# A decoder trunk on one core: treated K pairs in both output projections and in the attention's values

## The chip, the cores and the metric

The kernel runs on one core of a Trainium2 chip. The metric is device time in microseconds of one execution, as the median of several. Engines are named as in the profile: PE (TensorE, matmuls), PEld (its weight loads), DVE (VectorE), ACT (ScalarE), POOL (GpSimd) and SP (SyncE, which issues most DMAs).

## The reference

Two decoder layers over 256 tokens of width 2048, all in float32. Layer 0 mixes with a state space scan (SSD), layer 1 with differential attention; each is followed by a SwiGLU FFN, and every sub-layer has an RMSNorm before and after it.

```python
for i in range(DEPTH):                      # DEPTH = 2
    h = rmsnorm(x, norm_mix_pre[i])
    if i % 2 == 0:
        m = ssd_mixer(h, ssd_w_in, conv..., dt_bias, a_log, d, ssd_norm, ssd_w_out)
    else:
        m = diff_attention(h, da_w_qkv, lambdas..., da_subln, da_w_out, lambda_init)
    x = x + rmsnorm(m, norm_mix_post[i])
    h = rmsnorm(x, norm_ffn_pre[i])
    x = x + rmsnorm((silu(h @ w_gate) * (h @ w_up)) @ w_down, norm_ffn_post[i])

# the end of ssd_mixer: a gated RMSNorm in 8 groups, whose gain stands before the product
return (gv * rsqrt(mean(gv * gv) + eps) * norm_w) @ w_out          # 4096 -> 2048
# diff_attention: 16 heads, value width 128
q, k, v = split(u @ w_qkv)                                          # 2048 -> 3 x 2048
pr = softmax(q0 k0) - lam * softmax(q1 k1);  o = pr @ v
return (rmsnorm(o, subln_w) * (1 - lambda_init)) @ w_out            # 2048 -> 2048
```

## The kernel before

**Products.** Every matmul operand is split into a high part `hi` (float32r, a cast on ACT) and a low part `lo` (the rest, a subtraction on DVE). A product is three matmuls: high by high, high by low, low by high. `prep` (L126) splits a block of weights after its DMA, with a scale where one is given (L137, L138), else plainly (L133, L134). Weights come in blocks of 512 rows (four K tiles of 128) by 512 columns, 1 MB; a "chunk" is 512 output columns, a "K pair" two K tiles. The 256 tokens are two row tiles, t = 0 and 1.

**Three forms of a product.** `mv` (L177) does one chunk: the activations are stationary and the weights move; row tile 1 runs `lag` steps behind row tile 0 and the rest is carried over into the next product through the queue `pending`. `ws` (L201) has the weights stationary and gives the transposed result; queries and keys use it. `pair` (L220) does two chunks at once. In it, the K pairs named in `seven` are "treated": the four quarter products (2 row tiles by 2 chunks) of two K tiles are put together from seven products in place of eight, after a scheme of sums and differences. Such a K pair needs `form`s, that is sums and differences of the activations (`make_form`, L817: eight 128x128 operations on DVE and a split), and sums and differences of the weights: an accumulating DMA from the POOL queue (L247) and three additions on DVE (L261 to L263), then a second `prep`. Its extra products are gathered in four PSUM banks of the pool `auxp` (`cp` in the profile) and put together on DVE after the last treated K pair (L275 to L280). Before, the FFNs alone use `pair`, with K pairs 2, 4 and 6 treated for gate and up (`SEVEN`) and the lists in `PARTS` for the down projection.

**Order of work.** The emitted order is also the priority of the scheduler that lays out each engine's stream; it may let work that is ready go ahead of work that waits. `later(k, fn)` puts a piece of side work k steps on, `tick` counts steps, `lookup` runs such pieces early where their result is needed, and `flush` empties `pending`.

**The stages that the change touches.** The SSD output projection (`out_proj` with `w_so`) runs in two halves of K: the first half of all four chunks in the middle of the scan (L786), chunk 0 of the second half at its end (L788), and chunks 1 to 3 after the scan's pools are closed and others are opened (L848). Its activations are the pieces of `gate_group` (L615; `act_piece` transposes and splits them). The gain `ssd_norm` is applied to the weights. The last chunk ends in `norm_chain` (L642), which makes the residual and the next `xT`, the transposed activations, one row tile at a time; the sums of squares of the other chunks, with a product by the norm's gain on POOL (L688), are made by `sums` when a chunk is done.

In attention (L967), for each of four groups of four heads (`hg`): values by `mv`, then queries and keys by `ws`, then softmax and the rest as side work (`later`) under the next group's products. Value tiles lie in the pool `mpool` with two buffers. The output projection (L1071) is four chunks by `mv`.

Raw weight blocks have three buffers (`rawp`); while `deep` is set, in the FFN's middle, two of five go to `mpool` as well. The split tiles `hi` and `lo` have four buffers each.

## Time and profile before

| | |
|---|---|
| median of 3 runs | 2540.5 us (2540.33 to 2541.4) |
| profiled execution | 2541.16 us, span 2539.4 us |
| granted TensorE clock | 0.998 |
| PE busy | 2517.3 us, 11866 matmuls |
| DVE, ACT, POOL busy | 1901.7, 1364.6, 224.4 us |
| DMA | 536.16 MB, mean 211 GB/s |

The span reaches from the first instruction to the last; the profiled execution's time has 1.76 us around it. Busy time of PE is the union of overlapping matmuls, so it tells where TensorE had work, not at what pace. `acc`, `cp`, `hi`, `lo`, `raw` are tiles by the program's names, `ah_s`/`al_s`, `ah_f`/`al_f` and `ah_o`/`al_o` the high and low parts of the SSD's, the FFN's and the attention's activations. In time, the scan with the first half of the output projection takes the first 612 us, the rest of the output projection and the norm lie up to about 717 us, the first FFN up to about 1426, attention up to about 1759, its output projection and norm up to about 1825, and the second FFN the rest.

### The profile page before, as it was taken

The page shows a single profiled execution, that of the slowest core. Times are in us where ns is not written, and L with a number is a line of the kernel's source. Part 1 is how long each engine was busy: PE and PEld are TensorE (multiplying, and loading weights), DVE is VectorE, ACT ScalarE, POOL GpSimd, SP SyncE. Part 2 cuts the span into 40 slices and gives each one's busy share as a digit, 9 for nine tenths or more (in the row PEclk, how much of TensorE's full clock was granted, in tenths as well). Part 3 has the DMA queues.
Part 4 walks back from the last instruction along what each step waited for, and adds up shares of the span by engine and source line. Part 5 has one row for each costly group of instructions (what it writes and reads, how often), then busy time and mean ns, then how long its engine had stood idle before and what let it go on. Part 6 is the DMA issues. An engine that isn't in the chain of part 4 may idle for free.

```text
span 2539.4 us, 31214 instructions
## 1 busy us (share of the span) xinstructions
PE 2517.3 (99%) x11866; PEld 2071.8 (82%) x11866; DVE 1901.7 (75%) x2274; ACT 1364.6 (54%) x1655; POOL 224.4 (9%) x214
## 2 busy tenths in 40 slices
PE   9999999999999999999999999999999999999998
PEld 7877888788888888888888888887888888888886
DVE  6777547777687888977887765566688889878985
ACT  5767546665565454544454654455655454535453
POOL 0121000110110000001001100001100000010002
PEclk9999999999999999999999999999999999999999
DMA  7545555554776776778677544544666966796673
GB/s 279 197 167 183 186 194 199 166 183 171 257 261 211 254 238 210 235 230 244 209 239 243 189 150 166 183 151 156 241 222 201 292 213 214 234 264 207 211 251 146
DMA packets 141366, 536.16 MB, mean 211 GB/s; under 512 B 14176, under 2 KB 30880, under 8 KB 114208
## 3 DMA queue, kind: packets, MB, share of 16 engines
q1 hardware_dynamic: 125584, 502.91, 57.3%
q0 software_dynamic: 15264, 30.94, 6.4%
q8 instruction: 93, 1.52, 0.2%
q14 instruction: 57, 0.47, 0.1%
q10 hardware_dynamic: 368, 0.32, 0.0%
HBM read 516.22 MB, written 17.89 MB: 210 GB/s over the span
## 4 chain that ended last, share of the span: by engine, by line
PE 91%; DVE 3%; issue 2%; ACT 2%; DMA 1%; POOL 0%; SPq 0%; DVEq 0%; ACTq 0%; POOLq 0%
PE acc L238 36%; PE acc L187 35%; PE cp L238 7%; PE acc L212 5%; PE acc L214 2%; DVE lo L134 2%; ACT hi L133 1%; PE sc L1010 1%; PE pt_f L291 1%; PE py L565 1%; DMA mt<-acum_d 1%; PE ptx L658 0%; PE po L1046 0%; PE pc L472 0%; PE pt_s L291 0%
## 5 line engine op out<-in xcount | busy, mean ns | idle before, releaser
L134 DVE TENSOR_TENSOR lo<-raw,hi 128x2048 fp32r<-128x2048 f32 (+2 forms) x451 | 848.2, 1888 | 363.0 <-ACT hi L133 362.2
L133 ACT CAST hi<-raw 128x2048 fp32r<-128x2048 f32 (+2 forms) x451 | 699.9, 1558 | 592.0 <-DVE raw L263 189.2
L238 PE MATMUL acc<-hi,xT 128*128 128x512 f32 x1840 | 589.0, 390 | 0.0
L187 PE MATMUL acc<-hi,xT 128*128 128x512 f32 x1792 | 586.1, 399 | 0.6 <-ACT hi L133 0.5
L238 PEld LDWEIGHTS acc<-hi,xT 128*128 128x128 f32 x1840 | 345.3, 188 | 71.5
L187 PEld LDWEIGHTS acc<-hi,xT 128*128 128x128 f32 x1792 | 335.8, 188 | 74.1 <-issue 4.9
L238 PE MATMUL acc<-lo,xT 128*128 128x512 f32 x920 | 358.1, 389 | 0.0
L187 PE MATMUL acc<-lo,xT 128*128 128x512 f32 x896 | 352.3, 394 | 2.6 <-DVE lo L134 2.6
L133 ACT CAST hi<-rawm 128x2048 fp32r<-128x2048 f32 (+1 forms) x115 | 207.8, 1807 | 173.7 <-DVE rawm L263 108.3
L134 DVE TENSOR_TENSOR lo<-rawm,hi 128x2048 fp32r<-128x2048 f32 (+1 forms) x115 | 248.1, 2157 | 70.2 <-ACT hi L133 66.1
L238 PEld LDWEIGHTS acc<-lo,xT 128*128 128x128 f32 x920 | 172.7, 188 | 35.7
L187 PEld LDWEIGHTS acc<-lo,xT 128*128 128x128 f32 x896 | 169.0, 189 | 40.2 <-DVE lo L134 5.5
L238 PE MATMUL acc<-hi,ah_f 128*128 128x512 f32 x468 | 183.1, 391 | 0.0
L238 PE MATMUL acc<-hi,al_f 128*128 128x512 f32 x468 | 182.2, 389 | 0.0
L238 PE MATMUL acc<-lo,ah_f 128*128 128x512 f32 x468 | 182.1, 389 | 0.0
L212 PE MATMUL acc<-xT,hi 128*128 128x512 f32 x512 | 180.4, 398 | 0.0
L238 PE MATMUL cp<-hi,ff 128*128 128x512 f32 x468 | 156.8, 389 | 0.0
L214 PE MATMUL acc<-xT,lo 128*128 128x256 f32 x512 | 143.0, 280 | 0.0
L138 DVE SCALAR_TENSOR_TENSOR lo<-raw,cols,hi 128x512 fp32r<-128x512 f32 x128 | 92.5, 769 | 56.6 <-ACT hi L137 56.3
L137 ACT ACTIVATE hi<-raw,cols 128x512 fp32r<-128x512 f32 x128 | 84.6, 715 | 59.4 <-PE acc L187 39.3
L212 PEld LDWEIGHTS acc<-xT,hi 128*128 128x128 f32 x512 | 96.1, 188 | 22.8
L238 PEld LDWEIGHTS acc<-hi,al_f 128*128 128x128 f32 x468 | 87.8, 188 | 18.3
(279 smaller groups left out, 3469.9 us busy)
## 6 DMA issues: line engine op xcount, KB each, us to landing
raw<-in_w_zxbc_dram SPq DMA_DIRECT2D x77, 1024.0 KB, 4.8
raw<-in_w_d_dram SPq DMA_DIRECT2D x98, 512.0 KB, 5.8
raw<-in_w_g_dram SPq DMA_DIRECT2D x96, 512.0 KB, 6.0
raw<-in_w_u_dram SPq DMA_DIRECT2D x96, 512.0 KB, 5.8
raw<-in_w_qkv_dram SPq DMA_DIRECT2D x48, 1024.0 KB, 4.7
raw<-in_w_so_dram SPq DMA_DIRECT2D x32, 1024.0 KB, 4.8
rawm<-in_w_g_dram SPq DMA_DIRECT2D x64, 512.0 KB, 5.9
rawm<-in_w_u_dram SPq DMA_DIRECT2D x64, 512.0 KB, 6.0
```

The source lines that it names most:

```text
L133: nc.scalar.copy(hi, raw)
L134: nc.vector.tensor_tensor(lo, raw, hi.bitcast(F32), op=ALU.subtract)
L137: nc.scalar.activation(hi[:, j], raw[:, j], AF.Copy, scale=scale[j])
L138: nc.vector.scalar_tensor_tensor(lo[:, j], raw[:, j], scale[j], hi[:, j].bitcast(F32), op0=ALU.mult, op1=ALU.subtract)
L187: nc.tensor.matmul(acc[t], a, b[:, j], start=(i == 0 and j == 0 and q == 0), stop=(i == last and j == 1 and q == 2))
L212: nc.tensor.matmul(acc[ct], hi[:, j, cs], x.rearrange("p a s -> p (a s)"), start=(i == 0 and j == 0), stop=False)
L214: nc.tensor.matmul(acc[ct][:, :S], lo[:, j, cs], x[:, 0], start=False, stop=(i == last and j == 1))
L238: nc.tensor.matmul(acc[k], a, b, start=first and q == 0, stop=last and q == 2)
L291: nc.tensor.transpose(pt[:, j], src[:, j * P:(j + 1) * P], ident)
L565: nc.tensor.matmul(py[e * 64:(e + 1) * 64, a], xd[c][:, 2 * a + e], mts[c][:, 2 * a + e], start=True, stop=True)
L1010: nc.tensor.matmul(sc[c][:, h], qT[cp, h % 2, ts], kT[cp, h % 2, :nk * P], start=True, stop=True)
```

## The change

1. `ssd_norm` is no longer applied to the weights: `prep`, `halves` and `mv` lose their scale, and `act_piece` applies the gain to the transposed activations instead, in four operations of 128 columns on ACT and on DVE each (in place of one of 512).
2. In both output projections chunks 1 and 2 become a `pair` with three treated K pairs: 9, 11, 13 of 8 to 15 in the SSD's second half, 1, 3, 5 of 0 to 7 in the attention's. Chunk 0 goes before it and chunk 3 after it by `mv`. Their forms are made as side work of chunk 0 and lie in `xT`, which is idle at that time (`idle_xT`).
3. The values are made by `v_pair`, two groups at a time, with K pairs 4 and 6 treated: groups 0 and 1 ahead of the first queries, groups 2 and 3 between the third group's queries and its keys. The two forms are made in the first and used in both; they lie in a buffer of `mpool`. In the first, row tile 1 of K pairs 0 and 1 comes after row tile 0 of both (`lead`).
4. In these pairs the first sum of the weights is an addition on DVE (`chip`) in place of the accumulating DMA.
5. In a pair of the output projections, the sums of chunk 0 are made three steps into it and the third gain load follows one step later; the partial sum `p3` moves from the third chunk's end to wherever the third sum is made.

```diff
-    def prep(raw, scale=None):
+    def prep(raw):
...
+        nc.scalar.copy(hi, raw)
+        nc.vector.tensor_tensor(lo, raw, hi.bitcast(F32), op=ALU.subtract)
         return hi, lo
...
-    def pair(blocks, stat, seven, form, done):
+    def pair(blocks, stat, seven, form, done, lead=0, chip=False):
...
-            if kp in seven:
-
+            if kp in seven and chip:
+                nc.vector.tensor_tensor(raw[:, 0], raw[:, 0], raw[:, 1], op=ALU.add)
+            elif kp in seven:
                 nc.gpsimd.dma_start(raw[:, 0:1], src[0][:, 1:2], accum_op=ALU.add)
             if kp not in seven:
                 hi, lo = prep(raw)
-                for t in range(NT):
+
+                def block(t, kp=kp, hi=hi, lo=lo):
                     for c, e in ((0, 2), (1, 0)):
                         for j in range(2):
                             mm((t, c), stat(kp, j, t), hi[:, e + j], lo[:, e + j], kp == end and j == 1)
                         if kp == end:
                             done(t, c, acc[(t, c)], ss)
                     tick()
+
+                block(0)
+                if kp < lead:
+                    pending.append(lambda block=block: block(1))
+                    if kp == lead - 1:
+                        flush()
+                else:
+                    block(1)
                 continue
...
+        for sl in (slice(0, 4),) if scale.shape[1] == 1 else [slice(j, j + 1) for j in range(4)]:
+            sc = scale if scale.shape[1] == 1 else scale[:, sl]
+            nc.scalar.activation(hi[:, sl], pt[:, sl], AF.Copy, scale=sc)
+            nc.vector.scalar_tensor_tensor(lo[:, sl], pt[:, sl], sc, hi[:, sl].bitcast(F32),
+                                           op0=ALU.mult, op1=ALU.subtract)
...
+    def idle_xT(i):
+
+        return xT[i // 2][:, :, :, i % 2 * P:(i % 2 + 1) * P]
...
-            ssd_act[(t, g)] = act_piece(yf, f"s{g}_{t}")
+            ssd_act[(t, g)] = act_piece(yf, f"s{g}_{t}", scale=ssd_norm[:, 4 * g:4 * g + 4])
...
+            if 1 in two:
+
+                later(3, lambda: [row(t, 0) for t in range(NT)])
+                later(4, lambda: pw(2))
...
+                if first and last:
+                    nc.vector.tensor_tensor(m[k], ps, y, op=op)
+                    return
...
-    out_proj(w_so, False, False, ssd_act, list(range(8, 16)), 0, False, 1, None, None, ssd_norm, ns=range(0, 1))
+    sforms = {}
+    for k, kg in enumerate((9, 11, 13)):
+        later(2 + 2 * k, lambda k=k, kg=kg: make_form(
+            sforms, kg, act_stat(ssd_act), lambda name, shape: s2.tile(list(shape), F32, tag="t2", name=name), at=idle_xT(k)))
+    out_proj(w_so, False, False, ssd_act, list(range(8, 16)), 0, False, 1, None, None, ns=range(0, 1))
...
-    out_proj(w_so, False, True, ssd_act, list(range(8, 16)), 0, False, LAG2, t512, load_post(0), ssd_norm, ns=range(1, 4))
+
+    out_proj(w_so, False, True, ssd_act, list(range(8, 16)), 0, False, LAG2, t512, load_post(0), ns=(3,),
+             two={1: (9, 11, 13)}, forms=sforms)
...
+    def v_pair(hg, seven, lead=0):
+
+        def done(t, c, ps, ss):
+            if not c and not t:
                 vt = mpool.tile([P, 4, 512], F32, tag="m", name="v")
...
+            y, op = ss[(t, c)]
+            nc.vector.tensor_tensor(y, ps, y, op=op)
+            nc.scalar.activation(values[(hg + 1 - c, t)], y, AF.Copy, scale=lookup(rstd, (1, t)))
+
+        pair(twos(w_qkv, 8 + hg), kp_stat, seven, lambda kp, f: form_of(lookup(vforms, kp), f), done, lead, True)
...
+    for k, kp in enumerate((4, 6)):
+        later(6 + 3 * k, lambda k=k, kp=kp: values_forms(k, kp))
+    v_pair(0, (4, 6), LAG // 2)
...
     for hg in range(4):
+        attention_keys(hg, 0)
+        if hg == 2:
+
+            v_pair(2, (4, 6))
+        attention_keys(hg, 1)
         attention_group(hg)
-    out_proj(w_ao, True, True, att, list(range(8)), 2, False, LAG2, t512, load_post(2))
+    aforms = {}
+    for k, kg in enumerate((1, 3, 5)):
+        later(3 + 2 * k, lambda k=k, kg=kg: make_form(aforms, kg, act_stat(att), t512, at=idle_xT(k)))
+    out_proj(w_ao, True, False, att, list(range(8)), 2, False, LAG2, t512, None, ns=(0,))
+    out_proj(w_ao, True, True, att, list(range(8)), 2, False, LAG2, t512, load_post(2), ns=(3,),
+             two={1: (1, 3, 5)}, forms=aforms)
```

141 lines of the change are left out of this document (69 added, 72 removed).

## The prediction

> **What bounds the kernel now.** I read the parts of the page first, then the cores, the chain of work, the groups by form, and the windows of the stages that the change touches.
>
> ```profile
> PE 2517.3 (99%) x11866; PEld 2071.8 (82%) x11866; DVE 1901.7 (75%) x2274; ACT 1364.6 (54%) x1655; POOL 224.4 (9%) x214
> core 0: 2539.4 us, clock 0.998
> L238 PE MATMUL acc<-hi,xT 128*128 128x512 f32 x1840 | 589.0, 390 | 0.0
> 1894.04 6.12 PE acc L238 x27
> 624.12 73.49 PE acc L187 x324
> 1426.37 12.00 PE acc L187 x52
> 1438.36 0.44 PE pb L312 x4
> PE acc L187 <- DVE lo L134: 2.6, 5, 1.3
> ```
>
> PE is busy for all but 22 us of the span, at full clock, so TensorE's stream is the bound and a saving has to come out of it. The group row says 390 ns for a matmul, but neighbours overlap: the chain (start, length, count) passes 27 matmuls of L238 in 6.12 us and 324 of L187 in 73.49 us, both 0.227 us each. One matmul taken out is worth 0.227 us, not 0.390. A stage stays on that pace only while VectorE (DVE) and ScalarE (ACT) hand over the high and low parts in time; the last row shows that L187 waited for a low part only 2.6 us in the whole run.
>
> The windows give start:end, length, then busy time (and count) of PE, PEld, DVE, ACT, POOL, then clock, DMA share, GB/s.
>
> ```profile
> 832.60:874.00 41.40, 41.40 (x193) 34.43 (x192) 36.56 (x47) 17.61 (x14) 2.84 (x4) 1.00 0.72 246
> 612.00:633.50 21.50, 21.50 (x100) 17.79 (x99) 17.27 (x28) 17.00 (x29) 1.58 (x2) 1.00 0.57 185
> 633.50:675.00 41.50, 41.50 (x184) 34.35 (x183) 26.06 (x36) 22.87 (x40) 5.90 (x4) 1.00 0.81 304
> 1406.00:1431.30 25.30, 24.17 (x118) 18.59 (x117) 23.37 (x57) 21.33 (x57) 4.56 (x6) 1.00 0.46 166
> 1431.30:1459.00 27.70, 27.70 (x154) 24.05 (x153) 15.85 (x10) 13.74 (x9) 0.44 (x1) 1.00 0.64 228
> 1570.00:1612.00 42.00, 42.00 (x224) 34.32 (x224) 28.70 (x49) 24.45 (x48) 2.02 (x2) 1.00 0.38 131
> 1750.00:1800.00 50.00, 50.00 (x234) 41.28 (x233) 23.51 (x21) 23.58 (x27) 11.49 (x7) 1.00 0.52 185
> ```
>
> The first row is a pair of chunks in the FFN with three treated K pairs, as the change now makes elsewhere: DVE is busy 36.56 of 41.40 us and PE misses nothing. The second and third are the SSD output projection, the fourth is the norm between the first FFN and attention, where DVE is busy 23.37 of 25.30 us, the fifth the time in which the first values pair would finish, the sixth the third values chunk and what follows, the seventh the attention's output projection.
>
> **The matmuls.** A plain K pair over two chunks is 2 row tiles x 2 chunks x 2 K tiles x 3 products = 24 matmuls; a treated one is 7 x 3 = 21. Treated pairs added: three in the SSD output projection, three in the attention's, two in each of two values pairs: 10. 10 x 3 = 30 matmuls, 30 x 0.227 = 6.81 us off TensorE. Nothing else is added to PE: forms, chip additions and scales are on DVE and ACT.
>
> **What a treated pair costs beside PE.**
>
> ```profile
> L134 DVE TENSOR_TENSOR lo<-raw,hi 128x2048 fp32r<-128x2048 f32 x241 | 551.0, 2294 | 247.6 <-ACT hi L133 246.9
> L133 ACT CAST hi<-raw 128x2048 fp32r<-128x2048 f32 x241 | 458.8, 1912 | 410.9 <-DVE raw L263 189.2 <-PE acc L212 85.0 <-issue 40.5
> L134 DVE TENSOR_TENSOR lo<-raw,hi 128x1536 fp32r<-128x1536 f32 x50 | 87.6, 1752 | 18.9 <-ACT hi L133 18.9
> L133 ACT CAST hi<-raw 128x1536 fp32r<-128x1536 f32 x50 | 74.2, 1483 | 67.2 <-PE acc L238 39.2 <-issue 14.4 <-ACT hi L133 7.1
> L263 DVE TENSOR_TENSOR raw<-raw 128x512 f32<-128x512 f32 x50 | 34.2, 684 | 0.0
> L824 DVE TENSOR_TENSOR xf<-xT 128x128 f32<-128x128 f32 x24 | 5.3, 283 | 0.0
> L285 DVE TENSOR_TENSOR ff<-f,ff 128x512 fp32r<-128x512 f32 x18 | 12.3, 687 | 2.4 <-ACT ff L284 2.4
> 1016.58 2.29 DVE L134 TENSOR_TENSOR lo<-rawm,hi 128x2048 fp32r<-128x2048 f32 x1 [2.11 <-ACT hi L133]
> 1018.78 2.28 DVE L134 TENSOR_TENSOR lo<-raw,hi 128x2048 fp32r<-128x2048 f32 x1
> ```
>
> Plain pair on DVE: 2.29 us. Treated: 0.68 (the chip addition that stands in for the accumulating DMA) + 1.75 + 3 x 0.68 + 2.29 = 6.78 us. A form: 8 x 0.283 + 0.69 = 2.95 us. The last two rows, of a timeline, show the hole in a treated pair: before the second low part DVE waits 2.11 us for ACT's second cast. They also show a low part issued 2.20 us after the last one, so the 2.29 overlap a little.
>
> **First values pair.** Before, the four blocks of values 0 are 96 matmuls, and PE has them done when L312 starts at 1438.36.
>
> ```profile
> 1420.18 2.28 DVE L134 TENSOR_TENSOR lo<-raw,hi 128x2048 fp32r<-128x2048 f32 x1
> 1430.80 0.61 DVE L664 SCALAR_TENSOR_TENSOR xT<-ptx,cols,xT 128x128 fp32r<-128x128 f32 x2 [0.43 <-ACT xT L663]
> ```
>
> The fourth block's low part is made at 1420.18, and xT is complete at about 1431.3. In the new pair K pairs 0 to 3 are also 96 matmuls, so PE comes to treated pair 4 near 1438.4 and wants pair 6's second low part 21 + 24 + 9 = 54 matmuls later, at 1450.6. From 1431.3 DVE has 19.3 us for two forms (5.9), two treated pairs (13.6) and a plain one (2.3): 21.8, of which the 1.9 us that DVE idles in the fourth window could take some. So 19.9 in 19.3: 0.6 late, and two holes of 2.11 make it 4.8 late if nothing fills them. The overlap of neighbouring instructions (about 0.08 on some 30) pulls it the other way, to nothing. I take 1.5 late, nearest to the FFN row, where the holes are mostly filled, and keep 0 and 4.8. The queries behind it need only one low part at first. The shorter lead (2 K pairs of row tile 0 = 24 matmuls, 5.4 us, instead of five halves = 30, 6.8 us) is covered by K pair 2's row tile 0 if that is placed ahead; if not it costs up to 1.4, inside the same range. The second values pair has no forms to make and the sixth row leaves DVE 13 us idle: nothing. Moving the third queries ahead of it puts the second group's softmax under a queries product instead of under the pair; both keep PE full, nothing. Its two half loads per K pair cost SP one more issue:
>
> ```profile
> raw<-in_w_so_dram SPq DMA_DIRECT2D x32, 1024.0 KB, 4.8
> raw<-in_w_d_dram SPq DMA_DIRECT2D x98, 512.0 KB, 5.8
> wpost<-in_post_rows_dram SPq DMA_DIRECT2D x16, 256.0 KB, 4.9
> ```
>
> A K pair lands in 5.8 us with three buffers ahead of PE's 4.8 to 5.4 us each: nothing. The third wpost load now sits on SP behind the POOL product of row 0, with the next K pairs' loads queued after it; its cover is the K pairs already loaded (two, over 10 us): nothing, and up to its 4.9 us if they were used up.
>
> **SSD output projection.**
>
> ```profile
> L138 DVE SCALAR_TENSOR_TENSOR lo<-raw,cols,hi 128x512 fp32r<-128x512 f32 x128 | 92.5, 769 | 56.6 <-ACT hi L137 56.3
> L137 ACT ACTIVATE hi<-raw,cols 128x512 fp32r<-128x512 f32 x128 | 84.6, 715 | 59.4 <-PE acc L187 39.3 <-issue 13.1 <-DMA raw<-in_w_so_dram 7.0
> L134 DVE TENSOR_TENSOR lo<-raw,hi 128x1024 fp32r<-128x1024 f32 x160 | 210.4, 1319 | 96.5 <-ACT hi L133 96.4
> L664 DVE SCALAR_TENSOR_TENSOR xT<-ptx,cols,xT 128x128 fp32r<-128x128 f32 x96 | 27.8, 345 | 5.3 <-ACT xT L663 5.1
> L663 ACT ACTIVATE xT<-ptx,cols 128x128 fp32r<-128x128 f32 x96 | 29.3, 374 | 9.4 <-PE ptx L658 8.3 <-DVE xT L664 0.3
> L285 DVE TENSOR_TENSOR al_s<-pt_s,ah_s 128x512 fp32r<-128x512 f32 x16 | 10.9, 683 | 2.2 <-ACT ah_s L284 2.2
> L284 ACT CAST ah_s<-pt_s 128x512 fp32r<-128x512 f32 x16 | 9.3, 578 | 0.0
> ```
>
> The scale leaves the weights: a block of four on DVE falls from 4 x 0.77 = 3.08 to 2 x 1.32 = 2.64 us (2.29 where it is one piece), on ACT from 4 x 0.715 = 2.86 to about 2. It goes to 16 activation pieces, priced by the nearest shape: DVE 4 x 0.345 = 1.38 for 0.68, ACT 4 x 0.374 = 1.50 for 0.58. None of it is on PE's path before (no L138 in PE's waits), so the relief is worth nothing there; the added 0.7 and 0.9 us per piece can delay a low part in the scan: 0 to 1, I take 0.2.
>
> Chunk 0 also makes three forms: 17.27 + 8.9 - 4 x 0.44 + two late pieces 1.4 = 25.8 us of DVE for 21.5, a backlog of 4.3 if none is made in earlier idle time, 0 if all is. The pair then asks 5 x 2.29 + 3 x 6.78 + 4 x 0.68 = 34.5 us of 41, less than the FFN row's 36.56, which PE did not feel. I take 1.0, range 0 to 4.3. The attention's projection has the same pair, but the seventh row leaves DVE half idle for the forms: 0.1, up to 1.5.
>
> **A lock that speaks against it.** Row sums end in a POOL product (L688, 1.30 us); row 0's two now fall into the pair.
>
> ```profile
> 1376.79 3.80 POOL L688 TENSOR_TENSOR m<-m,wpost 128x512 f32<-128x512 f32 x3 [4.78 <-ACT junk L302]
> 1379.77 5.17 DVE L134 TENSOR_TENSOR lo<-raw,hi 128x2048 fp32r<-128x2048 f32 x2 [3.82 <-ACT hi L133]
> 1780.95 2.29 DVE L134 TENSOR_TENSOR lo<-raw,hi 128x2048 fp32r<-128x2048 f32 x1 [3.63 <-ACT hi L133]
> 1781.61 2.79 POOL L688 TENSOR_TENSOR m<-m,wpost 128x512 f32<-128x512 f32 x1 [7.17 <-ACT junk L302]
> ```
>
> Where the two meet, one waits: three POOL products alone take 3.80, but one begun under a low part takes 2.79, and two low parts behind a product take 5.17 instead of 4.49. If both products come first in each output pair, DVE loses 2 x 1.3 us per pair; at 34.5 + 2.6 = 37.1 of 41 that is at the FFN row's load, so I add nothing in the sum and keep it as a rival. The Trainium skill states this rule (SBUF — State Buffer, Who interferes with whom): a DVE instruction with two SBUF inputs and a GpSimd one that reads SBUF take turns at a shared port pair, each holding it for a whole instruction. The trace agrees, by the 2.79 and 5.17.
>
> **Sum.** -6.81 + 1.5 + 1.0 + 0.2 + 0.1 = -4.0 us. The profiled execution took 2541.16 us (span 2539.4 and 1.76 around it), the median of the runs is 0.66 lower: 2540.5 - 4.0 = 2536.5.
>
> **Rivals.** (a) *All of it is kept*: late parts cost under 1.7, 2533.7 to 2535.4. For it: the FFN row, with no PE wait at 88% DVE, and DVE idle for 11.9 of 27.7 us in the fifth window. Against: that idle time is what the forms and treated pairs fill. Chance 0.36. (b) *Partly given back*, the forecast, 2535.4 to 2540.5. Chance 0.43. (c) *The port pair takes the rest*: 2 x 2.6 us on top of the late parts in the two output pairs, so -4.0 + 5.2 = +1.2, 2541.7; it decides if DVE has no slack when row 0's products run. Chance 0.11. (d) *The treated pair is a serial chain*: cast 1.48, low part 1.75, additions 2.05, cast 1.91, low part 2.29 and the next plain pair's 2.29 make 11.8 us for PE's 10.2 (45 matmuls); 10 times 1.6 = 16 late, 2540.5 - 6.8 + 16 = 2549.7, slower. It decides from 1.2 us per treated pair on (11.9 in all). Against it: 1018.78 follows 1016.58 without a hole, and the FFN runs this pattern unhindered. Chance 0.10.
>
> About 0.2% (5.1 us) is what a measurement of this kernel can tell from no change: faster is below 2535.4, slower above 2545.6. Faster is (a), 0.36; slower most of (d), 0.09; same the rest, 0.43 + 0.11 + 0.01 = 0.55. The range goes from the full saving with a microsecond of old waits gone, 2532.8, to just past (c), 2542.5; that leaves out (d) and a little at either end. The forecast's own range is 2535.4 to 2540.5.
>
> **What would show it.** PE's count falls by 30; L137 and L138 have 0 instructions of the weights; the low part's waits in front of L238's matmuls between 1438 and 1460 are near 1.5 us, and near 1 between 633 and 675. Wrong if PE's waits for low parts grow by over 7 us, or by none.

## The result and the profile after

The changed kernel takes 2560.0 us (median of six runs, 2559.3 to 2562.7), the kernel before 2540.8 on the same chip: ratio 1.0077, interval 1.0064 to 1.009. The forecast was 2536.5, its range 2532.8 to 2542.5. So it is slower, by 19.3 us, where 4.0 were to be gained.

The page and the cores of the changed kernel, against the first two rows of the prediction:

```profile
PE 2519.5 (98%) x11836; PEld 2070.5 (81%) x11836; DVE 1973.4 (77%) x2400; ACT 1374.0 (54%) x1645; POOL 236.2 (9%) x214
core 0: 2559.2 us, clock 0.996
PE 61%; DVE 6%; issue 3%; ACT 2%; POOL 1%; DMA 1%; SPq 0%; DVEq 0%; ACTq 0%; POOLq 0%
```

The 30 matmuls are gone. But the span is 19.8 us longer, the mean clock is lower, and the chain that ended last (the third row) runs over PE for 61% of the span, before for 91%. To find the place, the run is cut at marks that both traces have: the SSD output projection from its first matmul in the second half of K to the first transpose of the new `xT`, and the attention's output projection from the last group's scores to the first transpose behind it. First the kernel before, then the changed one, in windows (columns as in the prediction):

```profile
612.10:698.30 86.20, 85.52 (x381) 70.43 (x381) 56.67 (x84) 50.74 (x85) 10.63 (x9) 1.00 0.68 243
1719.80:1815.70 95.90, 95.20 (x443) 76.34 (x442) 52.97 (x72) 48.93 (x77) 14.83 (x9) 1.00 0.48 168
```

```profile
612.70:708.50 95.80, 87.70 (x372) 69.17 (x370) 72.50 (x98) 48.98 (x56) 15.16 (x9) 0.98 0.62 218
1729.50:1835.60 106.10, 97.82 (x433) 77.13 (x432) 77.67 (x122) 53.01 (x80) 15.47 (x9) 0.97 0.44 153
```

The SSD projection grew from 86.2 to 95.8 us (+9.6), the attention's from 95.8 to 106.1 (+10.3); all the rest is the same to 0.1 us (2357.4 and 2357.3). Both stages do 9 matmuls fewer (the records show 9 and 10) and VectorE is busy for 16 and 25 us more. PE, which had under a microsecond idle in each, is idle for 8.1 and 8.3 us, and the clock fell below one. Adding the 18 matmuls that should have been saved (18 x 0.227 = 4.1 us), the two stages lost 24.0 us against the sum of matmuls: 15.0 as idle time of PE beyond that of before, 5.1 as clock (below), and the remaining 3.9 as busy time that stretched, which was not taken apart.

PE's waits in the SSD projection and then in the attention's, in the changed kernel (total, times, longest):

```profile
PE cp L233 <- ACT hi L132: 2.3, 2, 1.6
PE acc L181 <- DVE lo L133: 1.6, 2, 1.4
PE acc L233 <- ACT hi L132: 1.4, 3, 0.6
PE cp L233 <- DVE lo L133: 1.2, 1, 1.2
PE pt_s L297 <- ACT y L659: 1.0, 1, 1.0
...
PE pt_o L297 <- DVE ob L1093: 4.0, 2, 3.5
PE pp L1076 <- DVE e L1066: 1.9, 1, 1.9
```

With the smaller ones, not shown, the waits of each stage come to 8.2 and 8.3 us, which is all of PE's idle time there. In the SSD projection they are many small ones. In the attention's they fall on the last group's softmax, on `e` and `ob`, and hardly on the weights.

**Where the SSD projection goes wrong.** A timeline of POOL, VectorE and ScalarE in the changed kernel (start, length, instruction, idle time before it):

```profile
615.26 0.89 DVE L341 TENSOR_TENSOR xf<-ah_s,al_s 128x128 f32<-128x128 f32 x4
615.48 0.67 POOL L93 TENSOR_TENSOR rs_g<-ms_g,mhalf 128x1 f32<-128x1 f32 x1 [20.07 <-DVE ms_g L90]
...
620.92 0.15 DVE L90 TENSOR_SCALAR ms_g<-ssg 128x1 f32<-128x1 f32 x1
620.99 0.69 DVE L341 TENSOR_TENSOR xf<-ah_s,al_s 128x128 f32<-128x128 f32 x3
621.22 3.21 POOL L93 TENSOR_TENSOR rs_g<-ms_g,mhalf 128x1 f32<-128x1 f32 x1 [5.07 <-DVE ms_g L90]
622.80 1.22 DVE L133 TENSOR_TENSOR lo<-raw,hi 128x1024 fp32r<-128x1024 f32 x1
624.46 0.72 ACT L659 ACTIVATE y<-y,rs_g 128x512 f32<-128x512 f32 x1 [3.00 <-POOL rs_g L93]
626.42 0.35 DVE L307 SCALAR_TENSOR_TENSOR al_s<-pt_s,cols,ah_s 128x128 fp32r<-128x128 f32 x1 [2.40 <-ACT ah_s L306]
```

GpSimd's power of 128 numbers, the norm of the last group's second piece, takes 3.21 us (before 1.03): it starts inside a train of form instructions and ends only after VectorE's train of two-input instructions stops at 624.0. ScalarE waits 3.00 us for it, PE's transposes for ScalarE, VectorE 2.40 us for the activations, and the low parts queued behind that instruction start late, so that raw buffers come free late. In the kernels below that make the forms later this power takes 0.55 us. Not every train of sums does this: the first piece's power, the second row above, ran beside four sums and took 0.67. The prediction had the same lock between two-input VectorE and GpSimd instructions, but looked for it at the product of the row sums only.

**Where the attention's goes wrong.** The same view, VectorE at the last softmax, and last the second `ob` of the kernel before:

```profile
1757.48 0.89 DVE L341 TENSOR_TENSOR xf<-ah_o,al_o 128x128 f32<-128x128 f32 x4
1758.57 0.73 DVE L1064 TENSOR_SCALAR e<-e,sm,neglam 128x256 f32<-128x256 f32 x2
1760.21 2.29 DVE L133 TENSOR_TENSOR lo<-raw,hi 128x2048 fp32r<-128x2048 f32 x1
1762.41 0.28 DVE L344 TENSOR_TENSOR f<-xf,f 128x128 f32<-128x128 f32 x1
1762.62 0.68 DVE L1091 TENSOR_REDUCE sso<-ob 128x4 f32<-128x512 f32 x1
1770.55 0.69 DVE L1093 TENSOR_TENSOR ob<-po,rs_o 128x512 f32<-128x512 f32 x1 [0.90 <-POOL rs_o L93]
```

```profile
1757.11 0.69 DVE L1054 TENSOR_TENSOR ob<-po,rs_o 128x512 f32<-128x512 f32 x1 [1.19 <-POOL rs_o L93]
```

The forms (L341 to L345) and the treated K pair's additions stand between the steps of the softmax chain (`e`, `sso`, `ob`). From the last group's first scores, where the stage begins, to the start of the second `ob` 41.0 us pass (before 37.3). PE runs out of matmuls meanwhile and waits for `e` and `ob`: chunk 1's, which need no forms, used to be there.

**The clock.** Three times in the changed kernel's two stages the granted clock falls to half for 3.4 us. These are the 3.4 us ahead of each fall, and the fall (PEclk is the third number from the end):

```profile
661.97:665.38 3.41, 1.63 (x7) 0.82 (x6) 3.32 (x3) 2.33 (x2) 0.00 (x0) 1.00 0.16 66
665.38:668.80 3.42, 3.42 (x10) 2.65 (x9) 3.42 (x2) 0.00 (x0) 0.00 (x0) 0.50 0.78 244
1757.65:1761.06 3.41, 1.08 (x6) 0.40 (x4) 3.41 (x12) 3.41 (x7) 0.00 (x0) 1.00 0.00 0
1761.06:1764.48 3.42, 3.40 (x16) 3.40 (x17) 2.91 (x7) 1.07 (x2) 0.76 (x1) 0.50 0.31 73
1767.89:1771.30 3.41, 0.00 (x0) 0.00 (x0) 2.51 (x8) 0.54 (x1) 1.12 (x1) 1.00 0.08 31
1771.30:1774.72 3.42, 3.33 (x10) 2.89 (x11) 3.15 (x7) 1.24 (x2) 0.00 (x0) 0.50 0.00 0
```

Each of the three dips costs half of 3.4 us, that is 1.7 us, since PE is busy all through it; 5.1 together, about a fifth of the loss. Such waits of PE are thus paid for a second time. The Trainium skill (TensorE: Matmul & The Clock Gate, What's actually happening) describes a gate that halves the clock after an idle window of about 3.4 us and gives it back after a busy one. The length of the dips agrees, and so does the third one, which follows 3.4 us without a matmul; ahead of the first two PE was not idle for a whole window but busy for 1.63 and 1.08 of 3.41 us.

### The profile page after: what moved, and what is told of

Same layout as the page of the kernel before. It is cut to its first block, busy times and chain, and to the rows that moved or that the text cites. A ratio compares the mean times of both kernels' runs of the same rounds, so it can differ in the third digit from the quotient of the medians.

```text
span 2559.2 us, 31366 instructions
## 1 busy us (share of the span) xinstructions
PE 2519.5 (98%) x11836; PEld 2070.5 (81%) x11836; DVE 1973.4 (77%) x2400; ACT 1374.0 (54%) x1645; POOL 236.2 (9%) x214
## 4 chain that ended last, share of the span: by engine, by line
PE 61%; DVE 6%; issue 3%; ACT 2%; POOL 1%; DMA 1%; SPq 0%; DVEq 0%; ACTq 0%; POOLq 0%
PE acc L233 37%; PE cp L233 8%; PE acc L181 8%; PE acc L205 4%; DVE lo L133 3%; PE acc L207 2%; ACT hi L132 2%; PE sc L1049 1%; PE pt_f L297 1%; DMA raw<-in_w_ao_dram 0%; PE ptx L698 0%; DVE raw L267 0%; DVE raw L268 0%; DVE raw L269 0%; POOL rs_post L93 0%
## 5 line engine op out<-in xcount | busy, mean ns | idle before, releaser
L133 DVE TENSOR_TENSOR lo<-raw,hi 128x2048 fp32r<-128x2048 f32 (+2 forms) x516 | 949.1, 1848 | 382.9 <-ACT hi L132 377.0
L132 ACT CAST hi<-raw 128x2048 fp32r<-128x2048 f32 (+2 forms) x516 | 782.4, 1525 | 677.2 <-DVE raw L269 239.6
L233 PE MATMUL acc<-hi,xT 128*128 128x512 f32 x2060 | 661.0, 390 | 1.2 <-ACT hi L132 1.2
L181 PE MATMUL acc<-hi,xT 128*128 128x512 f32 x1536 | 501.6, 398 | 0.0
L233 PEld LDWEIGHTS acc<-hi,xT 128*128 128x128 f32 x2060 | 386.6, 188 | 81.7 <-ACT hi L132 2.0
L233 PE MATMUL acc<-lo,xT 128*128 128x512 f32 x1030 | 401.2, 389 | 0.1
L181 PE MATMUL acc<-lo,xT 128*128 128x512 f32 x768 | 301.2, 393 | 2.4 <-DVE lo L133 2.4
L133 DVE TENSOR_TENSOR lo<-rawm,hi 128x2048 fp32r<-128x2048 f32 (+1 forms) x112 | 242.3, 2164 | 58.8 <-ACT hi L132 55.1
L233 PEld LDWEIGHTS acc<-lo,xT 128*128 128x128 f32 x1030 | 193.4, 188 | 40.3 <-DVE lo L133 0.6
L233 PE MATMUL acc<-hi,ah_f 128*128 128x512 f32 x468 | 183.1, 391 | 0.0
L233 PE MATMUL acc<-hi,al_f 128*128 128x512 f32 x468 | 182.2, 389 | 0.0
L233 PE MATMUL acc<-lo,ah_f 128*128 128x512 f32 x468 | 182.1, 389 | 0.0
L233 PE MATMUL cp<-hi,ff 128*128 128x512 f32 x468 | 156.8, 389 | 0.0
L205 PEld LDWEIGHTS acc<-xT,hi 128*128 128x128 f32 x512 | 96.1, 188 | 23.6 <-issue 1.3
L233 PEld LDWEIGHTS acc<-hi,al_f 128*128 128x128 f32 x468 | 87.8, 188 | 18.4
L233 PEld LDWEIGHTS cp<-hi,ff 128*128 128x128 f32 x468 | 87.8, 188 | 18.0
L233 PEld LDWEIGHTS acc<-lo,ah_f 128*128 128x128 f32 x468 | 87.9, 188 | 17.8
```

The source lines that it names most:

```text
L132: nc.scalar.copy(hi, raw)
L133: nc.vector.tensor_tensor(lo, raw, hi.bitcast(F32), op=ALU.subtract)
L181: nc.tensor.matmul(acc[t], a, b[:, j], start=(i == 0 and j == 0 and q == 0), stop=(i == last and j == 1 and q == 2))
L205: nc.tensor.matmul(acc[ct], hi[:, j, cs], x.rearrange("p a s -> p (a s)"), start=(i == 0 and j == 0), stop=False)
L233: nc.tensor.matmul(acc[k], a, b, start=first and q == 0, stop=last and q == 2)
```

## The experiments

Each stage time is that of one profiled execution, cut at the same marks. Two kernels with the same SSD projection, the version with late loads and late forms and its SSD-only variant, differ by 1.0 us in it (90.9 and 89.9), which is how far these numbers can be trusted. The column "dips" has the number of stretches of 3.4 us at half clock in the SSD and in the attention's projection. Each is worth up to 1.7 us, and one more or less can be chance. The profiled executions of late forms, of one treated K pair and of three apart with early forms also have one in their first 140 us, where the source is the same for all. So the medians move less than the stages: from the changed kernel to late forms 7.5 us for 11.8. The ratios are to the kernel before, from runs side by side.

| kernel | SSD proj. us | att. proj. us | dips | median us | ratio, interval |
|---|---|---|---|---|---|
| before | 86.2 | 95.8 | 0, 0 | 2540.8 | |
| after | 95.8 | 106.1 | 1, 2 | 2560.0 | 1.0077, 1.0064 to 1.009 |
| values pairs only | 86.2 | 95.8 | 0, 0 | 2541.6 | 1.0002, 0.9993 to 1.0012 |
| no forms | 87.0 | 100.0 | 0, 0 | 2548.2 | 1.003, 1.0018 to 1.0041 |
| no sum on VectorE | 92.5 | 105.7 | 0, 3 | 2559.6 | 1.0072, 1.0057 to 1.0087 |
| plain K pairs first | 96.1 | 103.9 | 1, 2 | 2560.2 | 1.0074, 1.0059 to 1.0089 |
| one-input forms | 88.7 | 103.8 | 1, 2 | 2551.6 | 1.0042, 1.0027 to 1.0057 |
| forms on GpSimd | 96.7 | 110.7 | 2, 3 | 2567.7 | 1.0107, 1.009 to 1.0124 |
| late loads | 91.1 | 106.2 | 0, 3 | 2557.3 | 1.0064, 1.0049 to 1.0079 |
| late forms | 89.0 | 101.1 | 0, 1 | 2552.5 | 1.0045, 1.003 to 1.006 |
| late loads and forms | 90.9 | 101.1 | 0, 1 | 2552.6 | 1.0046, 1.0033 to 1.0059 |
| the same, sums by transfers | 88.9 | 100.2 | 0, 1 | 2551.3 | 1.0041, 1.0027 to 1.0055 |
| the same, two treated | 86.0 | 96.3 | 0, 0 | 2541.3 | 1.0002, 0.9993 to 1.0011 |
| the same, SSD only | 89.9 | 95.8 | 0, 0 | 2546.2 | 1.0022, 1.0012 to 1.0031 |
| three treated, apart | 88.3 | 97.5 | 0, 0 | 2545.8 | 1.0019, 1.001 to 1.0028 |
| two treated, all else as after | 91.5 | 98.4 | 1, 0 | 2549.7 | 1.0035, 1.0021 to 1.0048 |
| two treated, late, transfers | 85.4 | 95.5 | 0, 0 | 2541.2 | 1.0001, 0.9992 to 1.001 |
| one treated, late | 86.7 | 96.0 | 0, 0 | 2541.6 | 1.0004, 0.9995 to 1.0013 |
| three apart, early loads | 89.8 | 97.3 | 0, 0 | 2549.3 | 1.0034, 1.002 to 1.0049 |
| three apart, early forms | 91.9 | 103.3 | 1, 2 | 2553.8 | 1.0052, 1.0037 to 1.0067 |

By the sum of matmuls the two projections would be 84.2 and 93.8 us with three treated K pairs each, 84.8 and 94.4 with two, 85.5 and 95.1 with one.

### Which part of the change

**Values pairs only.** Both projections as four plain chunks again; the values pairs and the gain on the activations stay.

```diff
-    out_proj(w_so, ..., ns=(3,), two={1: (9, 11, 13)}, forms=sforms)
+    out_proj(w_so, ..., ns=range(1, 4))
-    out_proj(w_ao, True, False, att, ..., ns=(0,))
-    out_proj(w_ao, True, True, att, ..., ns=(3,), two={1: (1, 3, 5)}, forms=aforms)
+    out_proj(w_ao, True, True, att, list(range(8)), 2, False, LAG2, t512, load_post(2))
```

> Both output projections as four chunks without treated pairs, as before the change; the values in two pairs, the order of queries and keys, and the gain on the activation pieces stay. Stages are measured from the first SSD matmul of the second half to the first transpose of the norm (before 86.2 us, changed 95.8), from the first scores of the last attention group to the first transpose of its norm (before 95.9, changed 106.1), and attention between (before 312.8, changed 312.4). If the loss sits in the two output projections alone, this kernel has 86.2 and 95.9 again, keeps the 0.4 us gained in attention, and comes to 2540.0 to 2541.5. If the values pairs or the gain on the pieces cost something that the changed stages only show later, one of the two stages stays more than 2 us longer than before and the time is above 2543.

The time is that of the kernel before: the whole loss lies in the two projections. The attention stage with its twelve matmuls fewer (2.7 us) is 0.3 us shorter (312.9 to 312.6). PE's waits there, in this kernel, tell where the rest went:

```profile
PE pt_o L297 <- DVE ob L1089: 1.4, 3, 0.5
PE acc L233 <- ACT hi L132: 1.2, 2, 1.0
```

Neither wait was there before. The 1.2 us are the first values pair, the 1.4 the softmax ends of three groups.

**No forms.** The forms are not made; the treated products use plain activations in their place. Sums and differences of the weights stay.

```diff
-        later(2 + 2 * k, lambda k=k, kg=kg: make_form(sforms, ...))
-        later(3 + 2 * k, lambda k=k, kg=kg: make_form(aforms, ...))
-   lambda i, f: form_of(lookup(forms, kgs[i]), f)
+   lambda i, f: stat(kgs[i], 0, 0) if 1 in two else form_of(lookup(forms, kgs[i]), f)
```

> The changed kernel without the forms of the two output projections: their treated products use the plain activations instead, so about 18 us of VectorE work per three forms and its ScalarE casts fall away (it leaves that part of the computation out). If the forms are what holds VectorE up in front of the last attention group and at the end of the scan, both stages fall most of the way: from 95.8 to about 87 and from 106.1 to about 97, in all about 2543. If the wait is the treated weights' own chain or the loads, the stages lose at most 3 us each and the time stays above 2553.

The forms take 8.8 of the SSD's 9.6 us and 6.1 of the attention's 10.3. The three dips of the clock, 1.7 and 3.4 us of these, are gone with them. The forms are 3 x 2.95 = 8.9 us of VectorE work in each by the prediction's rows, so that the 18 us expected are those of both projections together; VectorE's busy time falls by 5.1 us in the SSD's (72.50 to 67.39) and 5.9 in the attention's (77.67 to 71.74). Removing them frees the softmax too, but both stages remain 2.8 and 6.2 us over the sum of matmuls, and the attention's 100.0 and the total are above the 97 and 2543 expected.

**No sum on VectorE.** In both projections the addition at L242 is left out, so the first product's weights lack their second chunk.

```diff
-            if kp in seven and chip:
-                nc.vector.tensor_tensor(raw[:, 0], raw[:, 0], raw[:, 1], op=ALU.add)
+            if kp in seven and chip:
+                if chip == 2:            # the values pairs alone
+                    nc.vector.tensor_tensor(raw[:, 0], raw[:, 0], raw[:, 1], op=ALU.add)
```

> The changed kernel without the first sum of the weights on VectorE in the two output projections (six additions of 0.69 us left out; the values pairs keep theirs). In the changed kernel VectorE stands at this addition for a load that has not landed (1.25, 3.05 and 1.33 us), with the sums of the pair before it queued behind. If that head of the queue is the cause, the SSD stage falls by 4 us or more and the attention's by about 1 to 2, in all about 2553. If it is not, each falls by no more than the additions themselves, and the time stays within 2 us of 2560.

3.3 us in the profiled SSD projection (1.7 of them a dip that this execution does not have), 0.4 in the attention's, and nothing that the medians tell from the changed kernel. Not the main cause.

**Plain K pairs first.** In the pairs, the order 8 10 12 9 14 11 13 15 and 0 2 4 1 6 3 5 7.

```diff
-    out_proj(w_so, False, True, ssd_act, list(range(8, 16)), ...
+    out_proj(w_so, False, True, ssd_act, [8, 10, 12, 9, 14, 11, 13, 15], ...
-    out_proj(w_ao, True, True, att, list(range(8)), ...
+    out_proj(w_ao, True, True, att, [0, 2, 4, 1, 6, 3, 5, 7], ...
```

> The changed kernel with the K pairs of both pairs in another order: three plain ones first, then treated, plain, treated, treated, plain (attention 0, 2, 4, 1, 6, 3, 5, 7; SSD the same plus 8, with 14 ahead of 11). Same work. If the stages lose because the treated pair comes second, before its forms and its split weights are ready, while the last group's chain still runs, the attention's stage falls by 5 us or more and the SSD's by 3 or more: 2552 or less. If the loss is the loads or VectorE's amount of work, the order changes neither by more than 2 us; two treated pairs in a row could cost 2 more.

+0.3 and -2.2 us, and 2560.2 in all. This order also puts the last two treated K pairs side by side, which later proved to cost something, so it does not acquit the order.

### Why the forms cost so much

**One-input forms.**

```diff
-                nc.vector.tensor_tensor(xf[:, t, j], hi.bitcast(F32), lo.bitcast(F32), op=ALU.add)
+                nc.vector.tensor_copy(xf[:, t, j], hi.bitcast(F32))
         # and likewise the four differences f[:, 0] to f[:, 3]; the two projections' forms alone
```

> Edit: the eight sums of each form of the two output projections become copies of their first operand: same number of VectorE instructions of the same size, but with one SBUF input instead of two (so the forms' values are not the reference's). Theory 1a (the two-input sums keep GpSimd's power for g7 from running, 3.21 us instead of 0.55, and ScalarE's activation, VectorE's low parts and SyncE's raw loads fall in line behind it): the power is back at about 0.55 us, the SSD projection falls from 95.8 us to 88 to 91, the attention's from 106.1 by under 2; total 2552 to 2555. Theory 1b (the time that the forms take in VectorE's queue counts, whatever their inputs): the SSD projection stays within 1.5 us of 95.8 minus what the copies are shorter, the total at 2557 to 2560 even if the power is short again.

The power for the last group falls from 3.21 to 1.44 us, not to 0.55, and the SSD projection by 7.1 us. A copy is also shorter than a sum (0.218 for 0.287 us), but 24 of them are only 1.7 us. So most of the SSD's loss came with the two inputs, as theory 1a had it. In the attention's projection 2.3 us went, little more than the shortening.

**Forms on GpSimd.**

```diff
-                nc.vector.tensor_tensor(xf[:, t, j], ...)       # and the four differences
+                nc.gpsimd.tensor_tensor(xf[:, t, j], ...)
```

> Edit: the forms' eight sums run on GpSimd instead of VectorE, their split stays where it was. Theory 1b (VectorE's queue): the attention's projection loses its 1.86 and 3.54 us waits on e and ob, falls from 106.1 us to 100 to 103; the SSD projection gains as well if GpSimd makes g7's power before the sums. Theory 1a (GpSimd is what is late): the power waits behind three forms of sums in GpSimd's own queue, SSD projection 96 to 105 us, total 2560 to 2570. Theory 4 (the forms wait for scratch tiles that the softmax holds): the attention's projection stays at 105 to 107.

Worse in both. PE's waits, SSD first:

```profile
PE pt_s L297 <- ACT y L660: 6.4, 1, 6.4
...
PE acc L181 <- ACT ah_o L306: 5.9, 1, 5.9
PE acc L181 <- DVE al_o L307: 3.2, 1, 3.2
```

The power now stands in GpSimd's queue behind the sums (it starts at 629.1 us instead of 621.2) and PE's transposes wait 6.4 us. In the attention's projection the waits on `e` and `ob` nearly vanish (1.9 and 4.0 to 0.2 and 0.2): they did come from the sums in VectorE's queue. But the split of the forms, which stays on VectorE, now waits for GpSimd's sums by way of ScalarE's cast, and the softmax's steps stand behind it. VectorE's largest wait in that stretch of this kernel, by its total:

```profile
DVE xT L291 <- ACT xT L290: 6.0, 2, 3.3
```

So the activations come 5.9 us late instead.

**Late loads.** The third gain load goes with chunk 3, the SSD's fetch of `x` behind its pair.

```diff
-                later(4, lambda: pw(2))
...
+        if 1 in two:
+            later(2, lambda: pw(2))
         for n in ns:
...
-    fetch_x(...)                                   # ahead of the SSD's pair
+             mid=lambda: fetch_x(...)              # an argument of its out_proj
```

> Edit: the third gain load is issued with chunk 3 instead of within the pair, and the SSD projection's fetch of x after its pair instead of before it. Theory 3 (transfers: x, the gain and the weights compete, VectorE's sums wait 1.25 and 3.05 us for the weights, SyncE holds weight loads behind the gain load 4.2 and 20.7 us): SSD projection falls from 95.8 to 91 to 93 us, the attention's from 106.1 to 103 to 105, total 2552 to 2556. Theories 1a and 1b (the forms): both within 1 us of 95.8 and 106.1, total 2558 to 2561.

The SSD projection is 4.7 us shorter, as theory 3 had it, though the power still takes 3.21 us there; 1.7 of the 4.7 are a dip that this execution does not have. The attention's is not shorter at all, as the others had it, and the total falls by 2.8 us only. In the attention's projection SyncE's gain load waited for the product of row 0 on GpSimd, with raw loads behind it; this is its row in the changed kernel (start, length):

```profile
1763.96 21.39 SPq L857 DMA_DIRECT2D wpost<-in_post_rows_dram  x2
1785.46 10.57 SPq L239 DMA_DIRECT2D raw<-in_w_ao_dram  x6
```

21 us without a raw load look alarming, and cost nothing that the comparison shows: PE is idle for 8.2 us in that stage with the gain load late, and for 8.3 in the changed kernel.

**Late forms.** Forms inside the pair, in the order of plain K pairs first; the SSD's scratch tiles for them come from another pool.

```diff
-        later(2 + 2 * k, lambda k=k, kg=kg: make_form(sforms, ...))       # in chunk 0
+        later(1 + 2 * k, lambda k=k, kg=kg: make_form(sforms, ...))       # in the pair
-        later(3 + 2 * k, lambda k=k, kg=kg: make_form(aforms, ...))
+        later(9 + 2 * k, lambda k=k, kg=kg: make_form(aforms, ...))
```

> Edit: the forms are made inside the pair (SSD: first at the pair's ticks 1, 3, 5; attention: at ticks 9, 11, 13 instead of 3, 5, 7), with the plain K pairs first so that the forms have time. Theory 1a and 1b alike (the forms stand in the way of g7's chain and of the last group's softmax): SSD projection 86 to 90 us, attention's 99 to 103 us, total 2543 to 2551. Theory 4 (the cover of plain matmuls is gone, and the treated K pairs cost VectorE and buffers wherever the forms are made): SSD above 92, attention above 103, total 2553 to 2560.

-6.8 and -5.0 us, one dip fewer in each: the stages fall as theories 1a and 1b had it, the total, 2552.5, lies between the theories. The place of the forms is half of the matter, and 3 to 5 us over plain chunks remain.

### What remains with the forms out of the way

**Late loads and late forms**, the two edits together, with no other:

> Edit: late loads and late forms together (gain load with chunk 3, x after the pair, forms inside the pair with the plain K pairs first). Theory 1+3 (two causes that each hold the same stages: the forms ahead of g7's chain and the softmax, and the loads behind the gain load and x): with the forms late, TensorE's wait at 1796 to 1798 us and the 1.7 us that the clock's dip to 0.53 to 0.62 costs behind it go, attention's projection 101.1 to 96 to 98 us; SSD 89.0 to 85 to 87 us; total 2542 to 2546. Theory 4 (treated pairs cost wherever the forms and the loads are): SSD over 88, attention over 100, total 2549 to 2553.

A miss: no better than late forms alone (90.9, which is 1.9 longer, and 101.1). I had taken the largest gap of the late-forms kernel, here with the dip of the clock behind it, for the effect of the gain load that holds the raw loads:

```profile
1796.00:1798.00 2.00, 0.00 (x0) 0.00 (x0) 0.08 (x1) 1.83 (x2) 0.00 (x0) 1.00 0.25 102
1798.00:1800.00 2.00, 1.88 (x5) 1.03 (x5) 1.90 (x1) 2.00 (x3) 0.00 (x0) 0.62 0.00 0
1800.00:1802.00 2.00, 2.00 (x5) 1.61 (x6) 2.00 (x2) 1.67 (x1) 0.00 (x0) 0.53 0.43 66
```

With the gain load out of the way the same wait is still there (PE at L233 on ScalarE's high part, 2.2 us), and ScalarE waits 6.4 us for VectorE's additions at L269.

**Sums by transfers**, on top of it:

```diff
-   ..., done, chip=1 in two)
+   ..., done)
```

> Edit: as the version with late loads and late forms, and the sums of the weight chunks made by accumulating transfers, as in the FFN, in place of VectorE's. If VectorE is what is still late in the pairs (12 sums and differences of 0.69 us each there, six of them these sums' and L267 to L269's neighbours): each projection 1 to 2 us shorter than with the sums on VectorE. If the transfers are (DMA share 0.9 to 1.0 in the stretches of the pairs): SSD 1 to 4 us longer, attention's the same or 1 us longer.

-2.0 and -0.9 us, the second within what one execution can tell: VectorE was what was late, not the transfers.

**Two treated K pairs** (11, 13 and 3, 5; order 8 10 12 9 11 14 13 15 and 0 2 4 1 3 6 5 7) in place of three:

```diff
-             two={1: (9, 11, 13)}, ...
+             two={1: (11, 13)}, ...
-             two={1: (1, 3, 5)}, ...
+             two={1: (3, 5)}, ...
```

> Edit: as the version with late loads and late forms, with two treated K pairs for three in each projection: one matmul pair's saving less in each (0.7 us), a third of the forms, sums and differences gone. If what is left over the sum of matmuls is due to the treated K pairs' own work, each projection is 0.5 to 2 us shorter than with three; if it is due to the missing cover of plain chunks or to the transfers, each is 0.5 to 0.7 us longer.

-4.9 and -4.8 us, far more than expected, and even with the kernel before. Either the third treated K pair costs that much, or the neighbourhood of two, since in this order no two stand side by side.

**SSD only**, the SSD projection of the version with late loads and late forms, the attention's as plain chunks:

```diff
-    out_proj(w_ao, True, False, att, ..., ns=(0,))
-    out_proj(w_ao, True, True, att, ..., ns=(3,), two={1: (1, 3, 5)}, forms=aforms)
+    out_proj(w_ao, True, True, att, list(range(8)), 2, False, LAG2, t512, load_post(2))
```

> Edit: the SSD projection with late loads and late forms, the attention's as four plain chunks again, values pairs kept. Attention's projection 95.8 us as before; SSD as in the first kernel of this call, 85 to 87 us under theory 1+3 (before 86.2), over 88 under theory 4; total 2538 to 2541 and 2541 to 2544.

89.9 and 95.8: the stages do not act on each other. The total, 2546.2, is above the 2541 to 2544 expected; 0.8 us of that lie in the norm and the FFN behind the SSD projection (709.4 for 708.6), of which more below.

**Three treated, apart**, which tells these two, again with late loads and late forms:

```diff
-    [8, 10, 12, 9, 14, 11, 13, 15]
+    [8, 10, 9, 12, 11, 14, 13, 15]
-    [0, 2, 4, 1, 6, 3, 5, 7]
+    [0, 2, 1, 4, 3, 6, 5, 7]
```

> Edit: the version with late loads and late forms, three treated K pairs, with a plain K pair between any two treated ones (K pairs in the order 8 10 9 12 11 14 13 15 and 0 2 1 4 3 6 5 7; in the version itself the second and third treated one stand side by side). Theory 5 (two treated K pairs in a row ask more of VectorE than their matmuls cover: by the rows 4 sums, 3 low parts, a form, about 8 us against 4.8 us of TensorE; one plain K pair between gives the time back): SSD projection 90.9 to 86 to 88 us, attention's 101.1 to 96 to 98 us, total 2541 to 2546. Theory 6 (it is the third treated K pair's work as such, VectorE's sum over the stage): both within 1.5 us of 90.9 and 101.1, total 2550 to 2554.

Both. Apart, three are 2.6 and 3.6 us better than side by side, and still 2.3 and 1.2 us worse than two. The windows of the pair in the SSD projection, first with three apart, then with two:

```profile
622.00:668.00 46.00, 43.86 (x194) 35.65 (x193) 41.34 (x61) 23.02 (x27) 3.08 (x2) 1.00 0.72 243
```

```profile
622.00:668.00 46.00, 46.00 (x206) 38.02 (x206) 37.23 (x49) 24.96 (x27) 4.69 (x2) 1.00 0.75 263
```

With three VectorE is busy for 90% and PE misses 2.1 us; with two, 81% and PE misses nothing. The FFN's pair, the prediction's measure, had 88% and a full PE, but one form was made in it where three are made here.

**Two treated, all else as in the changed kernel.**

```diff
-    enumerate((9, 11, 13)) ... two={1: (9, 11, 13)}
+    enumerate((11, 13)) ... two={1: (11, 13)}
-    enumerate((1, 3, 5)) ... two={1: (1, 3, 5)}
+    enumerate((3, 5)) ... two={1: (3, 5)}
```

> Edit: the changed kernel with its own order, loads and forms in chunk 0, but two treated K pairs for three in each projection. If the number is what decides (theory 6): SSD projection 95.8 to 86 to 89 us, attention's 106.1 to 96 to 99 us, total 2541 to 2548. If the place of the forms ahead of g7's chain and in the softmax decides (theories 1a and 1b): SSD 91 to 94 us, attention's 101 to 104 us, total 2550 to 2557.

91.5 and 98.4, and 2549.7 in all: early forms cost the SSD 5.5 us more than late ones even if there are only two (the late ones with late loads and plain K pairs first as well), the attention's 2.1. The SSD's time is the one expected if the place decides; the attention's lies between the two expectations.

**Two treated, late, sums by transfers** (the version with two, and the sums' edit above), and **one treated, late** (13 and 5, in the orders 8 9 10 11 12 14 13 15 and 0 1 2 3 4 6 5 7):

```diff
-             two={1: (11, 13)}, ...
+             two={1: (13,)}, ...
-             two={1: (3, 5)}, ...
+             two={1: (5,)}, ...
```

> Edit: late loads and forms, two treated K pairs in each projection, their weight sums made by accumulating transfers. With three treated ones the transfers' sums gave 2.0 us (SSD) and 0.9 us (attention). If VectorE still is late with two: SSD 86.0 to 84.8 to 85.6 us, attention's 96.3 to 95 to 96 us, total 2538 to 2540. If two leave VectorE time enough: both within 0.4 us, total 2540.5 to 2542.

> Edit: late loads and forms, one treated K pair in each projection (13 and 5). By the sum of matmuls 1.36 us less saved than with two in both together. If two treated ones are free of cost: total 2542 to 2543.5. If each treated one costs VectorE's queue what it saves: within 1 us of the version with two, 2540.5 to 2542.

85.4 and 95.5; 86.7 and 96.0; the totals, 2541.2 and 2541.6, cannot be told from the kernel before. One treated K pair loses about 1.0 us against the sum of matmuls per stage, two 1.2 to 1.9 (0.6 to 1.1 with the sums by transfers), three 3.7 to 4.1 if apart; the first two are near the 1.0 that one execution can tell. None of these versions beats the kernel before by anything measurable.

**Three apart, with one edit taken back each**, first the loads, then the forms (the diffs of late loads and of late forms, reversed):

> Edit: the version with three spaced treated K pairs and late forms (SSD projection 88.3 us, attention's 97.5), with the loads back where the changed kernel has them (gain load in the pair, x before it). If the loads count beside the forms (theory 3): SSD 91 to 94 us, attention's 99 to 102 us, total 2549 to 2555. If only the forms' place and the spacing count: both within 1 us of 88.3 and 97.5, total 2544 to 2548.

> Edit: the same version with the forms back in chunk 0 and the loads late. If the forms' place ahead of g7's chain and in the last softmax counts (theories 1a, 1b): SSD 91 to 94 us, attention's 102 to 106 us, total 2551 to 2557. If only the loads and the spacing count: both within 1.5 us of 88.3 and 97.5, total 2544 to 2549.

With the loads back the projections are 89.8 and 97.3: +1.5 and -0.2 us. The total is 3.5 us longer; 2.3 of it lie behind the SSD projection, from the first transpose of its norm to that of the next (710.9 for 708.6). There PE waits 1.4 us for a low part (it is busy for 2.57 of 4 us from 716 us on), and the clock falls to 0.59 over the next 4. The kernel with late forms has the same wait at the same place, 2.57 of 4 us, and a clock of 1.00 behind it (709.4).

With the forms back in chunk 0 the projections are 91.9 and 103.3: +3.6 and +5.8, and the power is back at 3.21 us. This is the cleanest price of the forms' place, as nothing else differs but the pool of the SSD's scratch tiles. The clock's dips are up to 1.7 of the 3.6 and up to 3.4 of the 5.8; the medians differ by 8.0 us.

## Why the prediction was wrong, step by step

- **The matmuls** were right: 30 fewer, at 0.227 us.
- **First values pair**, 1.5 late: PE waited 1.2 us for it. The size was right, but the wait is for ScalarE's high part, not for the low part that the sum and the sign named. That the second pair and the moved queries would cost nothing was wrong: 1.4 us of waits on `ob`, so that the values gained 0.3 us.
- **Gain on the pieces**, 0.2: the scan ends 0.6 us later (612.1 to 612.7), within its 0 to 1. But the same scan ends at 612.4 to 615.6 in the kernels above, so one trace each does not measure 0.2.
- **SSD: "I take 1.0, range 0 to 4.3"** is one of the two steps that failed. The stage lost 9.6 + 2.0 = 11.6 us. The step summed busy times: forms and low parts against 21.5 us of chunk 0, then the pair at 34.5 of 41. It did not ask what stood behind the forms in VectorE's queue and beside them on GpSimd: the last group's power (0.55 to 3.21 us), ScalarE's activation, the transposes and, through VectorE's low parts, the raw loads. The kernels with three K pairs apart divide the 11.6: 3.9 for the order and the loads (95.8 to 91.9), 3.6 for the place of the forms (91.9 to 88.3), and 4.1 that are left over the sum of matmuls. Other pairs of kernels give 0.2 to 6.8 us for the place of the forms (together with an order) and up to 4.7 for the loads, so these causes overlap.
- **Attention: "the seventh row leaves DVE half idle for the forms: 0.1, up to 1.5"** is the other. The stage lost 10.3 + 2.0 = 12.3 us: by the same kernels 2.8 for the order and the loads, 5.8 for the place of the forms, 3.7 left. The row ran from 1750 to 1800 us, and most of it lies behind the softmax. Cut where the chain ends, in the kernel before:

```profile
1719.80:1760.00 40.20, 40.20 (x201) 31.12 (x201) 27.13 (x54) 20.46 (x47) 2.02 (x2) 1.00 0.39 135
1760.00:1800.00 40.00, 40.00 (x177) 33.11 (x178) 19.21 (x11) 20.41 (x22) 9.48 (x5) 1.00 0.55 198
```

  VectorE is busy for 67% of the first half, in a chain whose steps PE waits for once its cover is used up; the forms have to be made there.
- **"The pair then asks 34.5 us of 41, less than the FFN row's 36.56, which PE did not feel"**: the amount was about right, the inference not. The pair's stretch in the changed kernel:

```profile
633.50:680.00 46.50, 41.62 (x170) 32.26 (x170) 32.55 (x28) 21.56 (x17) 4.41 (x2) 0.96 0.65 221
```

  VectorE is busy for 32.55 us, 70%, and PE misses 4.9 all the same. Where the pair makes its forms itself, VectorE is busy for 90% and PE misses 2.1. The average does not decide; side by side two treated K pairs cost 2.6 and 3.6 us more than apart (one dip of the clock in the second).
- **The third gain load**, "nothing, and up to its 4.9 us": it held SyncE for 21 us and cost nothing in the attention's projection. Right there, and not to be parted from `x` in the SSD's.
- **A term that was missing**: the clock, 3 x 1.7 = 5.1 us.

Of the rivals, the slower one (d, 2549.7) came nearest in time, still 10 us off, and not by its mechanism: of the 24 us lost, the 3.7 and 4.1 that stay with late forms, late loads and three apart are all that the treated K pair's own chain could explain. That it came near is luck. The lock of (c) is real, at another place than I priced. The sign I named for "wrong", PE's waits for low parts grown by over 7 us, did not appear. In the whole run of the changed kernel they are

```profile
PE acc L181 <- DVE lo L133: 4.0, 5, 1.6
...
PE cp L233 <- DVE lo L133: 1.7, 2, 1.2
```

5.7 us where there were 2.6. PE waited for the high part, `e`, `ob` and `y` as well. All its waits in the two stages add up to its idle time there, about 16.4 us, but that is less than the loss, as clock and stretched time come on top; the windows by stage show the loss, the waits for one kind of tile do not. Still open is how much of the SSD's loss the lock makes by itself: the copies, which bounded it, are also shorter and may be laid out differently, and with late loads the stage is 4.7 us shorter although the power is as long as ever. So are the 3.9 us of stretched time.

## What to carry to other kernels

Price side work by the queue that it enters and by the chain whose steps stand in it: ask which instruction comes next on that engine, who waits for it, and how much cover PE has just then. A window of busy shares answers this only if it is cut where the chain begins and ends. A saving of 0.7 us of TensorE per treated K pair is not worth 7.4 us more of VectorE (6.78 - 2.29 and a form of 2.95) where the forms are used once and VectorE carries the chain. In the FFN such K pairs run with PE full; no run here has the FFN without them, so what they are worth there is not shown.
